# Down and retention output products, weight sums and accumulators of a two-layer trunk regrouped

## The chip, the cores and the metric

One core of a Trainium2 chip runs the whole program. The engines are named as the profile names them: PE (TensorE, matrix products), DVE (VectorE), ACT (ScalarE), POOL (GpSimd) and SP (SyncE, which issues DMAs). The metric is the device time of one execution in microseconds; lower is better.

## The reference, cut to what matters

```
h = x                                            # 512 rows, 1024 columns
for i in range(2):
    hn = rmsnorm(h, mix_norm_g[i])
    h = h + (sgu_mixer(hn, ...) if i == 0 else retention(hn, ...))
    h = h + swiglu(rmsnorm(h, ffn_norm_g[i]), ffn_w_gu[i], ffn_w_down[i])
return rmsnorm(h, final_norm_g)

sgu_mixer: z = gelu(h @ w_in); u, v = split(z); v = layernorm(v)
           mixed = causal(w_s) @ v, per chunk of 128 rows and group; (u * (mixed + b)) @ w_out
retention: q, k, v, g = split(h @ w_in); 4 heads; (norm(scores(q, k) @ v) * silu(g)) @ w_out
           # w_out is 2048 x 1024
swiglu:    a, b = split(h @ w_gu); (silu(a) * b) @ w_down      # hidden 2816: w_down is 2816 x 1024
```

## The kernel before

Every product of two float32 matrices is made as three matmuls of rounded parts (`three`, L191 to L193): high by high, high by low and low by high. A weight arrives by a DMA that SP issues, as a tile of two k-tiles (128 x 2 x 512, 512 KB). `split` (L169, L170) copies its high part on ACT (`wh`) and subtracts on DVE for the low part (`wl`). All working tiles come from one pool of 38 buffers.

The program is a list of jobs that `pipeline` walks. Each job has a fetch (the DMA), a prep (the split) and a run (the matmuls). A fetch is written 8 weighted jobs ahead of its run, one that holds an accumulating DMA 12 ahead, and a prep 5 ahead. A scheduler then puts the instructions in a fixed order on each engine; an engine works through its own order and waits by semaphores.

Large products are made by `seven`: a 2 x 2 block product with seven half-size products (P1, P7, P6, Q4, P5, P2, P3) in place of eight. The weight side needs sums of blocks: P7 uses block 22 + 12, P6 that sum + 11, Q4 that sum + 21, and P5 uses 12 + 11. The left side needs such sums too (`combos`, made by DVE). A *step* is a pair of k-tiles in one product; each product has two steps, so a seven has 14 jobs. Seven is used for gate and up (`gu`, five units a layer, 24 matmuls of 256 columns a job), for v and g of each retention head (`vg`), for two thirds of the down product (`dn_0`, `dn_1`, 8 k-tiles each) and for half of the retention output (`ro0`, 8 k-tiles); the last three have 12 matmuls of 512 columns a job.

What is left of the down product (`dn_2`, 6 k-tiles: 4 of unit 4, 2 of the small first part `gl`) and of the retention output (`ro1`, 8 k-tiles) is made by `last_rows` with all eight block products, row chunk by row chunk, so that chunk 3 can be normalised while the others are still multiplied. Its accumulators are `ps_dn` and `ps_ro`. The same form makes the SGU output (`ps_so`).

Weight sums are made in two ways. In `gu`, DVE adds the blocks (L302) in the prep. In `vg`, `dn` and `ro0`, the sums of P7 and P5 are made by an accumulating DMA that POOL issues (L280) onto the loaded tile; P6 and Q4 are added by DVE.

PSUM is a pool of four tiles of 4 KB a partition, handed out by the scheduler as they come free.

In the SGU stage the order of code is: v's first half, its activation (`activate_v`, L703), v's second half, u's first half, `rowsum` (L799) with the bias sums `add_b` (L801), `mix` (L847) with `mx` (L849), u's second half, and the output projection.

Of the kernel before, what the change touches and what calls it, by code (L numbers as in the profile page):

```python
# [27 lines left out]
EARLY = 12  # L28
# [3 lines left out]
SUMS_X = ("P7", "P5")  # L32
SUMS_GU = ()
# [19 lines left out]
class Job:  # L53


    def __init__(self, fetch=None, prep=None, run=None, early=False):
        self.fetch, self.prep, self.run, self.early = fetch, prep, run, early


def pipeline(jobs):  # L60
    weighted = [j for j in jobs if j.prep is not None]
    n = len(weighted)
    e = f = p = 0
    done = 0
    for job in jobs:
        while e < n and e < done + EARLY:
            if weighted[e].early:
                weighted[e].fetch()
            e += 1
        while f < n and f < done + FETCH:  # L70
            if not weighted[f].early:
                weighted[f].fetch()
            f += 1
        while p < n and p < done + PREP:
            weighted[p].prep()
            p += 1
        if job.prep is not None:
            done += 1
        job.run()
# [3 lines left out]
def trunk(ctx, tc, x, positions, mix_g, ffn_g, fin_g, sgu_w_in, sgu_w_s, sgu_b_s, sgu_ln_g, sgu_ln_b,  # L83
# [8 lines left out]
    psp = ctx.enter_context(tc.tile_pool(name="psp", bufs=4, space=PSUM))  # L92
# [105 lines left out]
    def project_t(name, w, slices, evac, col_of=None, halves=False, mid=None):  # L198
# [30 lines left out]
        then(lambda: evac(ps))  # L229

    def project_n(name, w, slices, evac, col_of=None):
# [22 lines left out]
    PRODUCTS = ("P1", "P7", "P6", "Q4", "P5", "P2", "P3")  # L254

    def seven(name, w, groups, c1, c2, A, evac, mid=None, dma_sums=(), turned=False):
# [16 lines left out]

        def fetch(p, g, s, nk):
            def load(key, i, j):
                raw[key, g, s] = G(f"wr_{name}_{key}_{g}_{s}")
# [4 lines left out]

            if p == "P7":
                load("t", 1, 1)
                (onto if p in dma_sums else load)("t" if p in dma_sums else "o", 0, 1)
            elif p == "P1":
                load("b11", 0, 0)
            elif p == "Q4":
                load("b21", 1, 0)
            elif p == "P2":
                load("b21", 1, 0)  # L290
            elif p == "P5":
                load("b12", 0, 1)
                (onto if p in dma_sums else load)("b12" if p in dma_sums else "o", 0, 0)
            elif p == "P3":
                load("b22", 1, 1)

        def prep(p, g, s, nk):
            use = {"P1": "b11", "P7": "t", "P6": "t", "Q4": "t", "P5": "b12", "P2": "b21", "P3": "b22"}[p]
            extra = {"P7": "o", "P6": "b11", "Q4": "b21", "P5": "o"}.get(p)
            if extra and p not in dma_sums:  # L300
                d, o = raw[use, g, s][:, 0:nk, :], raw[extra, g, s][:, 0:nk, :]
                nc.vector.tensor_tensor(d, d, o, ALU.add)  # L302
            parts[p, g, s] = split(raw[use, g, s], f"{name}_{p}_{g}_{s}", nk)
# [22 lines left out]
        def run(i):  # L326
            p, (g, s, nk) = PRODUCTS[i // len(steps)], steps[i % len(steps)]
# [23 lines left out]
        for i in range(len(PRODUCTS) * len(steps)):
            p, st_ = PRODUCTS[i // len(steps)], steps[i % len(steps)]
            jobs.append(Job(lambda p=p, st_=st_: fetch(p, *st_), lambda p=p, st_=st_: prep(p, *st_), lambda i=i: run(i),
                            early=p in dma_sums))
# [51 lines left out]
    def into_x(p, acc, c):  # L406

        def plus(i, j, ps, op):
            q = X[:, 2 * i:2 * i + 2, j * T:(j + 1) * T]
            nc.vector.tensor_tensor(q, q, ps, op)  # L410

        if p == "P1":
            plus(0, 0, acc["X"], ALU.add)
        elif p == "P7":
            plus(1, 1, acc["Y"], ALU.subtract)
        elif p == "P6":
            plus(1, 0, acc["X"], ALU.add)
        elif p == "Q4":
            plus(1, 0, acc["Y"], ALU.add)
        elif p == "P5":  # L420
            plus(1, 1, acc["X"], ALU.subtract)
        elif p == "P2":
            plus(0, 0, acc["Z"], ALU.add)
        elif c == 1:
            plus(0, 1, acc["X"], ALU.subtract)

    lefts = {}

    def last_rows(name, w, raws, ready, mid=None):
# [48 lines left out]

        def start(kp, j):
# [9 lines left out]
        then(lambda: norm(3, ps[3]))  # L489
        for c in (2, 1, 0):  # L490
            then(lambda c=c: chunk(c, ends, (0,)))
            if c == 0:
                then(lambda: norm(0, ps[0], 0))
# [3 lines left out]
            then(lambda c=c: norm(c, ps[c], 1 if c == 0 else None))  # L497
        lefts[name] = left
# [23 lines left out]
    def rows_of(cols, dst, name):  # L522
# [11 lines left out]
        nc.vector.tensor_copy(dst, ps[:, 0, :])  # L534

# [583 lines left out]
```

## Time and profile before

| | |
|---|---|
| median of 3 runs | 1233.0 us (1232.68 to 1233.67) |
| the profiled execution | 1233.38 us |
| its span, first to last instruction | 1231.7 us |
| granted PE clock over the span | 0.999 |
| PE, DVE, ACT, POOL busy | 98%, 77%, 49%, 4% |

The span is what the trace covers; 1.7 us of the execution lie outside it. A busy share is the part of the span in which an engine ran an instruction; a weight load of PE runs beside its matmuls and is counted apart. Times in rows are microseconds, and a matmul's duration overlaps that of the next, so the pitch from start to start is what a matmul costs.

### The profile page before, as it was taken

To read this page: it belongs to the slowest core of one execution; us is meant where nothing else is said; L and a number is where in the kernel's file an instruction comes from. 1 tells how busy PE (TensorE), PEld (TensorE's weight loads), DVE (VectorE), ACT (ScalarE), POOL (GpSimd) and SP (SyncE) were. 2 spreads that over 40 slices of the span, in tenths; PEclk is the share of its full clock that TensorE was granted. 3 is DMA by queue.
4 is the path that set the end of the run, shared out by engine and by line. 5 is a ranking of instruction groups with operands and counts; after the bars stand their busy time and mean duration, and the time that the engine had idled before them with its cause. 6 is when DMAs were issued, how large, how long until landed. Compare 5 with 4: busy or idle time off the path is not lost.

```text
span 1231.7 us, 18116 instructions
## 1 busy us (share of the span) xinstructions
PE 1208.4 (98%) x7290; PEld 1079.0 (88%) x7290; DVE 946.9 (77%) x1092; ACT 608.5 (49%) x772; POOL 47.4 (4%) x49
## 2 busy tenths in 40 slices
PE   8999999999999999999999999999999999999997
PEld 6778899998999898988888888788899989998995
DVE  5599578879878976697483957996588799879864
ACT  4434356345544564556373545575454454446442
POOL 1000000000000001001000010100000100010000
PEclk9999999999999999999999999999999999999999
DMA  9312317766775767338174573665146667677711
GB/s 331 123 69 75 114 45 230 217 160 230 232 227 145 260 208 188 76 111 223 58 214 96 159 174 127 165 218 175 35 146 199 201 184 260 199 196 204 260 53 69
DMA packets 112868, 204.89 MB, mean 166 GB/s; under 512 B 7016, under 2 KB 20368, under 8 KB 112784
## 3 DMA queue, kind: packets, MB, share of 16 engines
q1 hardware_dynamic: 102864, 184.84, 45.9%
q0 software_dynamic: 9920, 18.90, 9.0%
q8 instruction: 57, 0.93, 0.3%
q14 instruction: 27, 0.22, 0.1%
HBM read 201.61 MB, written 2.10 MB: 165 GB/s over the span
## 4 chain that ended last, share of the span: by engine, by line
PE 86%; DVE 9%; ACT 3%; issue 2%; DMA 0%; SPq 0%; DVEq 0%; ACTq 0%
PE X_gu L193 6%; PE X_gu L192 6%; PE X_gu L191 6%; PE Y_gu L193 3%; PE Y_gu L192 3%; PE Y_gu L191 3%; PE X_vg L191 2%; PE X_vg L193 2%; PE X_vg L192 2%; PE ps_qk L192 2%; PE ps_qk L193 2%; PE ps_qk L191 2%; PE X_dn L191 2%; PE X_dn L192 2%; PE X_dn L193 2%
## 5 line engine op out<-in xcount | busy, mean ns | idle before, releaser
L170 DVE TENSOR_TENSOR wl_gu_P<-wr_gu_b,wh_gu_P 128x1024 fp32r<-128x1024 f32 x80 | 95.3, 1221 | 44.2 <-ACT wh_gu_P L169 43.7
L169 ACT ACTIVATE wh_gu_P<-wr_gu_b 128x1024 fp32r<-128x1024 f32 x80 | 80.3, 1050 | 8.0 <-PE X_dn L193 6.6
L169 ACT ACTIVATE wh_gu_P<-wr_gu_t 128x1024 fp32r<-128x1024 f32 x40 | 42.4, 1059 | 59.4 <-DVE wr_gu_t L302 58.2
L192 PE MATMUL ps_qk<-XL_r,wh_qk 128*128 128x512 f32 (+1 forms) x160 | 55.7, 348 | 0.6 <-DVE XL_r L584 0.6
L191 PE MATMUL ps_qk<-XH_r,wh_qk 128*128 128x512 f32 (+1 forms) x160 | 55.5, 349 | 0.0
L193 PE MATMUL ps_qk<-XH_r,wl_qk 128*128 128x512 f32 (+1 forms) x160 | 55.2, 348 | 0.0
L170 DVE TENSOR_TENSOR wl_gu_P<-wr_gu_t,wh_gu_P 128x1024 fp32r<-128x1024 f32 x40 | 48.1, 1220 | 4.6 <-ACT wh_gu_P L169 4.2
L170 DVE TENSOR_TENSOR wl_vg_P<-wr_vg_t,wh_vg_P 128x1024 fp32r<-128x1024 f32 x16 | 19.6, 1223 | 39.0 <-ACT wh_vg_P L169 37.8
L302 DVE TENSOR_TENSOR wr_gu_t<-wr_gu_t,wr_gu_b 128x1024 f32<-128x1024 f32 x40 | 47.6, 1218 | 0.1
L170 DVE TENSOR_TENSOR wl_vg_P<-wr_vg_b,wh_vg_P 128x1024 fp32r<-128x1024 f32 x32 | 38.2, 1221 | 10.0 <-PE X_vg L192 9.9
L191 PE MATMUL Y_gu<-xP7h_f,wh_gu_P 128*128 128x256 f32 x160 | 45.3, 283 | 0.0
L192 PE MATMUL Y_gu<-xP7l_f,wh_gu_P 128*128 128x256 f32 x160 | 45.3, 283 | 0.0
L193 PE MATMUL Y_gu<-xP7h_f,wl_gu_P 128*128 128x256 f32 x160 | 45.3, 283 | 0.0
L191 PE MATMUL X_gu<-xP6h_f,wh_gu_P 128*128 128x256 f32 x160 | 45.3, 283 | 0.0
L192 PE MATMUL X_gu<-xP6l_f,wh_gu_P 128*128 128x256 f32 x160 | 45.3, 283 | 0.0
L193 PE MATMUL X_gu<-xP6h_f,wl_gu_P 128*128 128x256 f32 x160 | 45.3, 283 | 0.0
L191 PE MATMUL Y_gu<-XH_f,wh_gu_Q 128*128 128x256 f32 x160 | 45.3, 283 | 0.0
L192 PE MATMUL Y_gu<-XL_f,wh_gu_Q 128*128 128x256 f32 x160 | 45.3, 283 | 0.0
L193 PE MATMUL Y_gu<-XH_f,wl_gu_Q 128*128 128x256 f32 x160 | 45.3, 283 | 0.0
L191 PE MATMUL X_gu<-xP5h_f,wh_gu_P 128*128 128x256 f32 x160 | 45.3, 283 | 0.0
L192 PE MATMUL X_gu<-xP5l_f,wh_gu_P 128*128 128x256 f32 x160 | 45.3, 283 | 0.0
L193 PE MATMUL X_gu<-xP5h_f,wl_gu_P 128*128 128x256 f32 x160 | 45.3, 283 | 0.0
(544 smaller groups left out, 4319.1 us busy)
## 6 DMA issues: line engine op xcount, KB each, us to landing
wr_gu_b<-in_ffn_w_gu SPq DMA_DIRECT2D x100, 512.0 KB, 3.8
wr_gu_o<-in_ffn_w_gu SPq DMA_DIRECT2D x40, 512.0 KB, 4.7
wr_dn_b<-in_ffn_w_down SPq DMA_DIRECT2D x40, 512.0 KB, 4.5
wr_vg_b<-in_ret_w_in SPq DMA_DIRECT2D x40, 512.0 KB, 4.2
wr_gu_t<-in_ffn_w_gu SPq DMA_DIRECT2D x20, 512.0 KB, 4.2
wr_qk<-in_ret_w_in SPq DMA_DIRECT2D x32, 256.0 KB, 4.1
wr_dn<-in_ffn_w_down SPq DMA_DIRECT2D x12, 512.0 KB, 4.1
wr_ro_b<-in_ret_w_out SPq DMA_DIRECT2D x10, 512.0 KB, 4.8
```

The costliest lines, as they stand in the source:

```text
L169: nc.scalar.activation(h, s, AF.Copy)
L170: nc.vector.tensor_tensor(l, s, f32(h), ALU.subtract)
L191: nc.tensor.matmul(o, ah, bh, start=start, stop=False, skip_group_check=True)
L192: nc.tensor.matmul(o, ah, bl, start=False, stop=False, skip_group_check=True)
L193: nc.tensor.matmul(o, al, bh, start=False, stop=stop, skip_group_check=True)
L302: nc.vector.tensor_tensor(d, d, o, ALU.add)
```

## The change

Four things change together.

1. `dn_2` and `ro1` are gone as `last_rows`. The second part of the down product is one seven of two groups (k-tiles 8 to 15, and the six of unit 4 and `gl`): four steps, 28 jobs, seven of them half as long. The retention output is one seven of two groups (16 k-tiles): four steps, 28 jobs. The normalisation of row chunks goes into the evacuations of these sevens (`into_x` with `norm`).
2. Weight sums by accumulating DMA, in place of DVE: `gu` and `vg` have P7 and P5 so, and Q4 is added onto P6's tile after P6's split. `dn_0` has P7, P6 (two adds, one after the other), P5 and Q4. `dn_1` and `ro` have P7 and P5, and P6 and Q4 are added onto the tile of the product before, after its split. An add is written 8 jobs ahead of its product, a second one onto the same tile 3 jobs earlier, and the load 2 earlier still; an add onto a split tile stands in that tile's prep.
3. The order of products is P1, P7, P6, P2, P5, Q4, P3 in `gu`, `vg` and `dn_0`; `dn_1` and `ro` keep the old one.
4. PSUM tiles are four fixed buffers, given out in the order of code, the longest free first (`ps_free`, `done`). `activate_v(0, ...)` becomes a job, so that it stands behind the first five preps.

Per step of seven jobs, DMAs of 512 KB, plain loads + accumulating adds:

| | before | after |
|---|---|---|
| gu | 8 + 0 | 5 + 3 |
| vg | 6 + 2 | 5 + 3 |
| dn_0 | 6 + 2 | 6 + 5 |
| dn_1 | 6 + 2 | 5 + 4 |
| ro | 6 + 2 (ro0) | 5 + 4 |

In all, 36 accumulating DMAs become 152, and matmuls of 512 columns fall by 60 (dn 36 over the two layers, ro 24).

```
-EARLY = 12
+ADD = 8
+STEP = 3
+LOAD = 2
...
-SUMS_X = ("P7", "P5")
-SUMS_GU = ()
...
+            if p in dma_sums:
+                n = len(bs) - 1
+                return [(ADD + STEP * (n - 1) + LOAD, first)] + [
+                    (ADD + STEP * (n - 1 - i), lambda b=b: add(p, b, g, s, nk)) for i, b in enumerate(bs[1:])]
...
             parts[p, g, s] = split(raw[p, 0, g, s], f"{name}_{p}_{g}_{s}", nk)
+            for q in onto:
+                if FROM[q] == p:
+                    add(p, BLOCKS[q][-1], g, s, nk)
...
     def PS(name, shape=(P, 2, T)):
-        return psp.tile(list(shape), F32, tag="ps", name=name)
+
+        s = ps_free.pop(0)
+        t = psp.tile(list(shape), F32, tag=f"ps{s}", name=name)
+        ps_held.append((t, s))
+        return t
+
+    def done(*tiles):
+
+        for t in tiles:
+            i = next(i for i, (u, _) in enumerate(ps_held) if u is t)
+            ps_free.append(ps_held.pop(i)[1])
...
-    activate_v(0, vps)
+    then(lambda: (activate_v(0, vps), done(*vps)))
...
+    def into_x(name, w, groups, A, ready=None, mid=None):
...
+            seven(name, w, groups, 0, T, A, evac, mid, ("P7", "P5"), onto=("P6", "Q4"))
+        else:
+            seven(name, w, groups, 0, T, A, evac, mid, ("P7", "P6", "P5"), order=LATER, onto=("Q4",))
...
-        down(1)
-        unit(4, {("P2", i): lambda i=i: lefts[f"dn{l}_2"](0, 1 - i) for i in range(2)})
-        last_rows(f"dn{l}_2", ffn_w_down[l], [(lambda i: he[i], [20, 21]), (lambda i: hq[4][i], t[4])], ready)
+        unit(3)
+        unit(4, {("P2", 1): lambda: A[1]("P1", 0), ("P5", 0): lambda: A[1]("P7", 0), ("P3", 0): lambda: A[1]("P6", 0)})
+        into_x(f"dn{l}_1", ffn_w_down[l], [(t[2], t[3]), ([16, 17, 20], [18, 19, 21])], A[1], ready)
...
-    last_rows("ro1", ret_w_out[0], [(lambda i, hd=hd: zq[hd][i], list(range(4 * hd, 4 * hd + 4))) for hd in (2, 3)],
-              normed("f1", ffn_g[1:2], raw_copy("f1")))
+    into_x("ro", ret_w_out[0], [(t[0], t[1]), (t[2], t[3])], outA, normed("f1", ffn_g[1:2], raw_copy("f1")),
+           {("P1", 1): heads[3][3], ("P7", 1): heads[3][2]})
```

**PE in the SGU stage.** `rowsum` and the `mix` tiles are PSUM tiles, and so are `ps_u_0` and `ps_u_1`, the accumulators of u; a number behind a name tells one tile from another. Before, PE has:

```order
L799 MATMUL rowsum<-wst,ones 128x512 x2
L847 MATMUL mix_783<-wst,v_0_324 128x128 x2
L847 MATMUL mix_783<-wst,v_0_329 128x128 x2
L847 MATMUL mix_795<-wst,v_0_324 128x128 x2
L847 MATMUL mix_795<-wst,v_0_329 128x128 x2
L191 MATMUL ps_u_0_833<-XH_in,wh_u_0_527 128x512
L192 MATMUL ps_u_0_833<-XL_in,wh_u_0_527 128x512
```

After, it has:

```order
L864 MATMUL rowsum<-wst,ones 128x512 x2
L913 MATMUL mix_783<-wst,v_0_393 128x128 x2
L913 MATMUL mix_783<-wst,v_0_398 128x128 x2
L913 MATMUL mix_996<-wst,v_1_545 128x128 x2
L913 MATMUL mix_996<-wst,v_1_550 128x128 x2
L913 MATMUL mix_795<-wst,v_0_393 128x128 x2
L913 MATMUL mix_795<-wst,v_0_398 128x128 x2
L913 MATMUL mix_1008<-wst,v_1_545 128x128 x2
L913 MATMUL mix_1008<-wst,v_1_550 128x128 x2
L913 MATMUL mix_783<-wst,v_0_393 128x128 x2
L913 MATMUL mix_783<-wst,v_0_398 128x128 x2
L913 MATMUL mix_795<-wst,v_0_393 128x128 x2
L913 MATMUL mix_795<-wst,v_0_398 128x128 x2
L203 MATMUL ps_u_0_833<-XH_in,wh_u_0_527 128x512
```

All eight groups of `mix`, in four tiles, now stand ahead of u's second half; before, two tiles stood ahead of it and the others behind its first accumulator.

**POOL's queue of accumulating DMAs at the first down product (`dn0_0`).** A name says which tile is added onto: before, `t` is P7's and `b12` is P5's, for each of the two steps; after, `P622` is the tile that was loaded with block 22 for P6. Before, these four are the program's first, and those of the second down product (`dn0_1`) follow:

```order
L280 DMA wr_dn0_0_t_0_0_2302<-in_ffn_w_down 128x2x512
L280 DMA wr_dn0_0_t_0_2_2338<-in_ffn_w_down 128x2x512
L280 DMA wr_dn0_0_b12_0_0_2502<-in_ffn_w_down 128x2x512
L280 DMA wr_dn0_0_b12_0_2_2543<-in_ffn_w_down 128x2x512
L280 DMA wr_dn0_1_t_0_0_3505<-in_ffn_w_down 128x2x512
```

After, twelve of gate and up (six a unit) stand ahead, and the first down product has ten:

```order
L295 DMA wr_dn0_0_P622_0_0_2315<-in_ffn_w_down 128x2x512
L295 DMA wr_dn0_0_P622_0_2_2348<-in_ffn_w_down 128x2x512
L295 DMA wr_dn0_0_P722_0_0_2350<-in_ffn_w_down 128x2x512
L295 DMA wr_dn0_0_P622_0_0_2315<-in_ffn_w_down 128x2x512
L295 DMA wr_dn0_0_P722_0_2_2389<-in_ffn_w_down 128x2x512
L295 DMA wr_dn0_0_P622_0_2_2348<-in_ffn_w_down 128x2x512
L295 DMA wr_dn0_0_P512_0_0_2532<-in_ffn_w_down 128x2x512
L295 DMA wr_dn0_0_P622_0_0_2315<-in_ffn_w_down 128x2x512
L295 DMA wr_dn0_0_P512_0_2_2590<-in_ffn_w_down 128x2x512
L295 DMA wr_dn0_0_P622_0_2_2348<-in_ffn_w_down 128x2x512
```

P6's two tiles get their first add, then the second beside P7's one, and last the one of Q4, beside P5's. POOL issues in this order, so that an add that waits (for its tile's load, for the add before onto it, or for the split) holds up those behind it.

**ACT at v's activation.** The tiles `wh_v` are the high parts of v's second half's weights. Before, ACT has:

```order
L173 ACTIVATE wh_v_3_246<-wr_v_3_244,mix_cols 128x512 x2
L670 ACTIVATE xq_294,ss_96<-X 128x1024
L703 ACTIVATE v_0_324<-ps_v_0_121,ry_n_2_318 128x512 x2
L703 ACTIVATE v_0_329<-ps_v_1_122,ry_n_2_318 128x512 x2
L173 ACTIVATE wh_v_0_373<-wr_v_0_357,mix_cols 128x512 x2
L173 ACTIVATE wh_v_1_379<-wr_v_1_359,mix_cols 128x512 x2
```

After, it has:

```order
L185 ACTIVATE wh_v_3_246<-wr_v_3_244,mix_cols 128x512 x2
L735 ACTIVATE xq_294,ss_96<-X 128x1024
L185 ACTIVATE wh_v_0_363<-wr_v_0_347,mix_cols 128x512 x2
L185 ACTIVATE wh_v_1_369<-wr_v_1_349,mix_cols 128x512 x2
L185 ACTIVATE wh_v_2_375<-wr_v_2_351,mix_cols 128x512 x2
L185 ACTIVATE wh_v_3_381<-wr_v_3_353,mix_cols 128x512 x2
L185 ACTIVATE wh_u_0_387<-wr_u_0_355,mix_cols 128x512 x2
L768 ACTIVATE v_0_393<-ps_v_0_121,ry_n_2_318 128x512 x2
L768 ACTIVATE v_0_398<-ps_v_1_122,ry_n_2_318 128x512 x2
```

The two activations of v have moved behind five weight copies.

## Rows read from the trace of the kernel before

**Rows 1.** The page's first part: busy us (share of the span), instructions, by engine.
```profile
PE 1208.4 (98%) x7290; PEld 1079.0 (88%) x7290; DVE 946.9 (77%) x1092; ACT 608.5 (49%) x772; POOL 47.4 (4%) x49
```

**Rows 2.** The page's chain that ended last: share of the span by engine.
```profile
PE 86%; DVE 9%; ACT 3%; issue 2%; DMA 0%; SPq 0%; DVEq 0%; ACTq 0%
```

**Rows 3.** TensorE's waits: us in total, times, longest us.
```profile
PE Y_dn L193 <- DVE h_Q4l L397: 2.5, 4, 0.6
...
PE ps_v L191 <- ACT wh_v L173: 2.0, 1, 2.0
...
PE ps_gl L192 <- DVE XL_f L584: 1.7, 4, 0.6
...
PE Y_ro L191 <- ACT wh_ro_P L169: 1.6, 1, 1.6
...
PE ps_dn L191 <- DVE X L554: 1.0, 1, 1.0
```

**Rows 4.** Windows: busy us of PE, PEld, DVE, ACT, POOL; PEclk, DMA share, GB/s.
```profile
185.00:265.00 80.00, 80.00 (x669) 80.00 (x668) 64.53 (x58) 40.97 (x41) 3.63 (x3) 1.00 0.67 206
...
266.00:307.00 41.00, 40.37 (x204) 34.02 (x203) 38.41 (x36) 20.91 (x22) 1.21 (x1) 1.00 0.73 216
```

**Rows 5.** The timeline of TensorE in the SGU output projection: start us, us.
```profile
149.68 0.39 PE L192 MATMUL ps_so<-wl_so,so_h 128*128 128x512 f32 x1
...
154.21 0.40 PE L191 MATMUL ps_so<-wh_so,so_h 128*128 128x512 f32 x1
```

**Rows 6.** TensorE's matmul groups of ps_dn and of ps_ro, by line: duration ns min/median/max.
```profile
L191 PE MATMUL ps_dn<-wh_dn,dn_h x96: 389/389/501, 466.5 to 1223.5; 128*128 128x512 f32 x96
...
L191 PE MATMUL ps_ro<-wh_ro,ro_h x64: 389/389/497, 838.2 to 883.1; 128*128 128x512 f32 x64
```

**Rows 7.** The timeline of PE at Q4 of the first down product: start us, us.
```profile
286.52 0.50 PE L192 MATMUL Y_dn<-wl_dn_Q,h_Q4h 128*128 128x512 f32 x1
...
287.65 0.50 PE L193 MATMUL Y_dn<-wh_dn_Q,h_Q4l 128*128 128x512 f32 x1 [0.63 <-DVE h_Q4l L397]
```

**Rows 8.** Groups by line and form, DVE and POOL: busy us, mean ns.
```profile
L302 DVE TENSOR_TENSOR wr_gu_t<-wr_gu_t,wr_gu_b 128x1024 f32<-128x1024 f32 x40 | 47.6, 1218 | 0.1
...
L280 POOL DMA_DIRECT2D wr_dn_t<-in_ffn_w_down x8 | 9.6, 1200 | 538.5 <-DVE wl_gu_Q L170 528.7 <-DMA wr_dn_t<-in_ffn_w_down 9.7
```

**Rows 9.** The timeline of PE and DVE at the SGU's mixing: start us, us.
```profile
86.28 1.95 PE L847 MATMUL mix<-wst,v 128*128 128x128 f32 x16
...
88.79 0.47 PE L191 MATMUL ps_u<-XH_in,wh_u 128*128 128x512 f32 x1 [0.56 <-DVE add_b L801]
...
86.48 2.16 DVE L801 SCALAR_TENSOR_TENSOR add_b<-rowsum,gains_cols,add_b 128x128 f32<-128x128 f32 x8 [1.37 <-PE rowsum L799]
...
88.56 0.68 DVE L833 TENSOR_TENSOR ur<-ps_u,R 128x512 f32<-128x512 f32 x1
...
89.16 1.40 DVE L849 SCALAR_TENSOR_TENSOR mx<-mix,gains_cols,add_b 128x512 f32<-128x512 f32 x2
...
91.07 1.42 DVE L838 TENSOR_TENSOR y<-u,mx 128x256 f32<-128x256 f32 x4
...
92.41 1.22 DVE L170 TENSOR_TENSOR wl_so<-wr_so,wh_so 128x1024 fp32r<-128x1024 f32 x1
```

**Rows 10.** The timeline of DVE at the end of the program: start us, us.
```profile
1221.92 1.41 DVE L1081 SCALAR_TENSOR_TENSOR o<-X,nf_dn,g_fin 128x512 f32<-128x512 f32 x2
...
1224.39 0.69 DVE L554 TENSOR_TENSOR X<-X,ps_dn 128x512 f32<-128x512 f32 x1 [1.06 <-PE ps_dn L193]
```

**Rows 11.** The page's DMA queues: packets, MB, share of the 16 engines' span.
```profile
q1 hardware_dynamic: 102864, 184.84, 45.9%
...
q0 software_dynamic: 9920, 18.90, 9.0%
```

**Rows 12.** The DMA issues: KB each, median us to landing.
```profile
wr_gu_b<-in_ffn_w_gu SPq DMA_DIRECT2D x100, 512.0 KB, 3.8
...
wr_dn_t<-in_ffn_w_down POOLq DMA_DIRECT2D x8, 512.0 KB, 9.2
```

More of the change, by code (lines that the diff above doesn't have):

```diff
@@ L53, with __init__ @@
 class Job:
-    def __init__(self, fetch=None, prep=None, run=None, early=False):
-        self.fetch, self.prep, self.run, self.early = fetch, prep, run, early
+    def __init__(self, fetch=None, prep=None, run=None):
+        self.run = run
+        self.steps = [] if prep is None else (fetch if isinstance(fetch, list) else [(FETCH, fetch)]) + [(PREP, prep)]
 def pipeline(jobs):
-    weighted = [j for j in jobs if j.prep is not None]
-    n = len(weighted)
-    e = f = p = 0
+    weighted = [j for j in jobs if j.steps]
+    leads = sorted({n for j in weighted for n, _ in j.steps}, reverse=True)
+    at = dict.fromkeys(leads, 0)
     done = 0
     for job in jobs:
[L66 to L77, printed above, removed]
+        for n in leads:
+            while at[n] < min(len(weighted), done + n):
+                for m, step in weighted[at[n]].steps:
+                    if m == n:
+                        step()
+                at[n] += 1
+        if job.steps:
             done += 1
@@ L297, in prep, with load @@
-        def prep(p, g, s, nk):
[L298 to L303, printed above, removed]
+        def load(p, b, g, s, nk):
+            raw[p, b, g, s] = G(f"wr_{name}_{p}{b}_{g}_{s}")
+            nc.sync.dma_start(raw[p, b, g, s][:, 0:nk, :], source(b, g, s, nk))
@@ L339, in run @@
                     evac(p, acc, None)
+                    if p in closes:
+                        done(acc[chain[p]])
             elif n < len(steps) - 2:
@@ L347, in run @@
                     evac(p, acc, c)
+                done(acc["X"])
             if mid and (p, n) in mid:
                 mid[p, n]()
[L351 to L354, printed above, removed]
+        for i in range(len(order) * len(steps)):
+            p, st_ = order[i // len(steps)], steps[i % len(steps)]
+            jobs.append(Job(fetch(p, *st_), lambda p=p, st_=st_: prep(p, *st_), lambda i=i: run(i)))
     def rows(k0, n):
@@ L492, in last_rows @@
             if c == 0:
-                then(lambda: norm(0, ps[0], 0))
+                then(lambda: add(0, 0))
             if c < 2:
@@ L496, in last_rows @@
             then(lambda c=c: chunk(c, ends, (1,)))
[L497 to L498 removed]
+            then(lambda c=c: add(c, 1 if c == 0 else None))
     def rsqrt_cols(src, n, scale, name):
```

222 lines of the change are left out of this document (135 added, 87 removed).

## The prediction

> **What bounds the kernel.** I read the busy shares first. TensorE (PE) runs 98% of the span, VectorE (DVE) 77% [rows 1]: the kernel is bound by PE, and less than 2% of the span can be won from waits. The chain that ended last says the same, with PE at 86% and DVE at 9% [rows 2]; the 9% are stretches where PE's next matmul came from a late DVE. The list of PE's waits then tells what can be won besides matmuls: Q4 of the down products four times for DVE's low part of a left side, the second half of v once for a weight copy on ACT, the retention output once, the four transposes ahead of a gate/up stage for `XL_f`, and the last chunk for DVE's addition into X [rows 3]. No large wait is put down to a weight's DMA, though the DMA engines are busy 67% and 73% of the time in gate/up and in the first down product [rows 4]. So matmuls taken away count in full, work taken from DVE counts only where PE waits for DVE, and DMA work added costs nothing until it makes a weight late.
>
> **Fewer matmuls.** Successive 512-column matmuls start 4.53 us apart over 20 of them, so one costs 0.2265 us [rows 5]. `ps_dn` has 96 matmuls on each of three lines, 144 a layer, and `ps_ro` 64 on each, 192 [rows 6]. In seven products, the six k-tiles of `dn_2` need 7/8 of 144 = 126, and the eight of `ro1` 168. That is 2 x 18 + 24 = 60 fewer, **-13.6 us**. They lie on PE's own path, so nothing hides this gain.
>
> **Q4's wait.** Between two matmuls of Q4 that should start 0.23 us apart stand 1.13 us [rows 7]: 0.9 us lost, four times [rows 3], 3.6 us. DVE was late because of its own weight additions for P6 and Q4 (L302, 1.22 us each [rows 8]). All of these go from the down products, and more than 0.9 us stood ahead of each Q4. **-3.6 us** (bounds 0 and -3.6: DVE's evacuations of PSUM into X stay). In gate/up DVE loses 60 additions, 73 us over the program, but PE does not wait for DVE there, so I take nothing.
>
> **Retention output.** Its P7 waited 1.6 us for ACT [rows 3]. With two groups, P1 has 24 more matmuls, 5.4 us, but the copy still stands behind a left-side copy on ACT which DVE feeds. I leave 0.4 of the wait: **-1.2 us** (bounds 0 and -1.6).
>
> **The SGU stage.** Two things change order. ACT's copies of v's next weights stand ahead of v's activation, so the 2.0 us wait for `wh_v` [rows 3] goes: -2.0 us. Against that, the fixed PSUM buffers put all mixing ahead of u's second half. Before, `ps_u` started 2.31 us after DVE had begun `add_b`, whose end it waited for [rows 9]. After, its buffer is that of a `mix` tile, free when DVE has read that tile a second time. By DVE's order that reading comes behind `add_b`, one `ur`, two `mx`, four `y`, a small operation and one `wl_so`. From the starts in [rows 9]: `add_b` 2.08 us, `ur` 0.60, `mx` 1.31, `y` 1.34, `wl_so` 1.14, the third `mx` 0.70, the small one an estimated 0.4, together 7.6 us. So u's second half starts 5.3 us later; but sixteen more mixing matmuls are done by then that used to come later, near 1.8 us (as many took 1.95 before, the overlap at their end included), so 3.5 us are lost. The output projection behind it needs DVE's `y` and ACT's copies, which slide too; I put 1 us on it (0 to 2). Net -2.0 + 3.5 + 1.0 = **+2.5 us** (from -2.0, if DVE runs so far ahead that `ps_u` loses nothing, to +5, if v's wait stays and the projection slides by 1.5).
>
> **Transitions and the tail.** Ahead of the first q/k product and of the second gate/up, the low part of the last transposed chunk is waited for, 0.4 us each as for `ps_gl` [rows 3]. The normalisation now hangs on evacuations with more DVE work between, a little more each, **+0.6 us** for both (0 to 2). At the end, DVE finishes two output pieces of another chunk, 1.41 us [rows 10], and by the new order such a pair stands ahead of the last addition into X, which was not held up before: **+1.0 us** (0 to 1.4).
>
> **DMA.** From the queues' shares of 1231.7 us [rows 11]: 45.9% for 184.84 MB is 1.60 us of all 16 engines for a 512 KB load; 9.0% for 36 accumulating ones is 3.08 us each, 1.92 times as much. Per step of seven products, with 168 matmuls of 256 columns at 80/669 us each [rows 4], a gate/up step is 20.1 us of PE; a down step of 84 matmuls is 19.0 us. Gate/up goes from 8 loads, 12.8 us (64%, and the window shows 67%) to 5 loads and 3 adds, 17.2 us (86%); `vg` comes to the same 17.2 us, 91% of 19.0. `dn_0` goes to 6 loads and 5 adds, 25.0 us in 19.0: **131%**. `dn_1` and `ro` come to 20.3 us, 107%. So the DMA engines fall behind in `dn_0` by 6.0 us a step, 12 us in all, and in `dn_1` and `ro` by about 1.3 us a step, 5 us in four.
>
> Whether PE feels it depends on the lead. An add is written 8 jobs ahead: 8 x 12 x 0.2265 = 21.7 us. An add lands 9.2 us after its issue [rows 12], the copy on ACT and the subtraction on DVE take an estimated 2.3 us (the latter as in [rows 8]), so some 10 us are left for a backlog that grows to 12 us only at the stage's end, where gate/up with its 86% follows and lets it shrink. P6, with two adds behind one another, has its load and first add earlier still. I take waits of **+1.0 us** in all (bounds 0 and 28: twice the 12 us of `dn_0`, and 4 us more behind them).
>
> The Trainium skill speaks against adds from POOL: its page "SBUF — State Buffer", section "SBUF: two separate sides", says that such a DMA's descriptors can't be written while DVE runs an operation in a two-port mode. Here POOL's issue of an add takes 1.20 us on the mean [rows 8], in stages where DVE is busy 81% to 94% of the time [rows 4]; the row shows no such stall. What it would make of the time stands with rival 2.
>
> **The sum.** Against the profiled execution of 1233.4 us: -13.6 - 3.6 - 1.2 + 2.5 + 0.6 + 1.0 + 1.0 = -13.3, so 1220.1; the median of the runs lies 0.4 us below that execution, so **1219.7 us**. The unknown small terms at their bounds, without the DMA's, give 1212 to 1228.
>
> **Rivals.** (1) *The DMA engines become the bound* (the other sign). In `dn_0` each step asks for 131% of them. If the backlog comes on top of one left by gate/up at 86%, or if contention stretches the landing beyond the 21.7 us of lead, every further microsecond of backlog is one of PE. It decides from a landing of about 19 us on, twice what [rows 12] shows. With the leads used up, 2 x 12 + 4 = 28 us less the 1.0 in the sum: about 1247 us; with half of it, 1233. For it: the sums above, the adds' double price. Against it: no wait for a weight's DMA now at 73%. (2) *Adds late in part.* In `dn_1` and `ro` an add onto a split tile can be issued only after that split, and POOL issues in order, so one waiting add holds the next ones. P6's add is written with P7's prep, 9 jobs or some 22 us ahead of P6's run; the split ahead of it (2.3), its landing (9.2) and its own split (2.3) take 14 us, and a queue of three adds of 3.08 us the rest. Waits of 1 to 2 us at some six places, in place of the 1.0 of the sum: 1225 to 1231 us. By the skill's rule the adds of a step would come later by up to 1.2 us each, 6 us for the five of `dn_0`; the time would be this rival's, and I count 0.03 of its chance to that. (3) *The SGU stage and the joints cost nothing*: DVE's freed time lets `ps_u` start in time and the tail stays: -13.6 - 3.6 - 1.6 - 2.0 + 1.0 gives 1213 us. (4) *The gains do not come*: `ro` and `dn_1` are closed by DVE's evacuations with norms, PE waits there for left sides as it did for Q4, 3 to 4 us in each of three sevens: 1229 to 1232 us.
>
> **How the numbers follow.** Forecast 0.54, rival 3 0.12, rival 2 0.14, rival 4 0.08, rival 1 0.12. A change of 0.2%, 2.5 us, is about what measuring this kernel can tell from none. Below 1230.5 lie the forecast, rivals 3 and 2 and a little of 4: 0.80; within 2.5 us of 1233 the rest of 4 and a half-sized rival 1: 0.08; above 1235.5 the rest of rival 1: 0.12. The range of 8 in 10 leaves out rival 1 and the upper part of 4, and the very lowest: 1213 to 1231.
>
> **What would show it.** Right: PE busy near 1194 us; no wait of Q4 for `h_Q4l`; `wh_v` gone from the waits; a new wait of `ps_u` of some 3 to 4 us for DVE's `mx`; q0 with about 79 MB at near 38% of the engines. Wrong: PE waits in `dn_0`, `dn_1` or `ro` for ACT's `wh_dn_P` or `wh_ro_P` whose releaser is a DMA (rivals 1, 2), or for DVE's `X` or left sides in the two-group sevens (rival 4).

## The result and the profile after

The changed kernel takes 1236.3 us in the median of 20 runs (1232.6 to 1238.6); the kernel before takes 1233.1 us in 20 runs beside it (1232.2 to 1234.4). The ratio is 1.0021, with a 95% interval of [1.0013, 1.0029]: slower by 0.2%, where 1.1% faster was forecast. The profiled execution took 1234.2 us with a span of 1232.5 us. One execution of one experiment below (PSUM as one pool) took 1975 us at a mean granted clock of 0.558, which nothing here explains, and is left out of its numbers.

The page of the changed kernel, its busy times, its DMA queues and its chain that ended last, against [rows 1], [rows 11] and [rows 2]:

```profile
PE 1198.6 (97%) x7230; PEld 1067.0 (87%) x7230; DVE 876.8 (71%) x1053; ACT 644.4 (52%) x832; POOL 184.6 (15%) x165
...
q0 software_dynamic: 40448, 77.63, 37.9%
q1 hardware_dynamic: 84176, 148.66, 35.8%
...
PE 74%; issue 7%; DMA 7%; DVE 5%; POOL 3%; ACT 2%; SPq 0%; POOLq 0%; DVEq 0%; ACTq 0%
```

PE has the 60 matmuls fewer and DVE is 70 us less busy. The accumulating queue q0 takes 37.9% of the DMA engines, as worked out ahead. But the chain now runs through DMA (7%), POOL (3%) and "issue" (7%), where before it had 2% of "issue" and none of the others. The waits of PE, against [rows 3] (us in total, times, longest us):

```profile
PE mix L913 <- DVE add_b L866: 2.2, 1, 2.2
PE ps_gl L204 <- DVE XL_f L648: 2.0, 4, 1.0
PE ps_gl L203 <- ACT XH_f L647: 2.0, 1, 2.0
PE X_dn L205 <- DVE h_P5l L427: 1.7, 4, 0.6
PE ps_u L203 <- DVE mx L915: 1.6, 1, 1.6
PE X_dn L203 <- ACT h_P5h L426: 1.4, 2, 0.7
PE X_ro L203 <- ACT z_P5h L426: 1.3, 1, 1.3
PE X_dn L204 <- DVE wl_dn_P L182: 1.3, 2, 0.8
PE ps_qk L203 <- ACT XH_r L647: 1.3, 1, 1.3
...
PE Y_ro L203 <- ACT sg L1085: 1.1, 1, 1.1
...
PE Y_dn L205 <- DVE h_Q4l L424: 0.9, 1, 0.9
```

The wait for `wh_v` is gone; Q4 waits once, not four times. In their place stand many small waits of the two-group sevens, for P5's left sides and weights. None of them names a DMA. One step further down, ACT's own waits do (three of the rows that name a DMA):

```profile
ACT wh_dn_P L181 <- DMA wr_dn_P<-in_ffn_w_down: 27.6, 12, 4.6
...
ACT wh_dn_Q L181 <- DMA wr_dn_P<-in_ffn_w_down: 13.8, 8, 3.0
...
ACT wh_ro_P L181 <- DMA wr_ro_P<-in_ret_w_out: 11.5, 4, 4.6
```

How a late add reaches PE is seen in ACT's timeline at P5 of dn_1 in the first layer (start us, us, in brackets the idle time before and what ended it), and in the chain of the same stretch:

```profile
464.58 1.06 ACT L181 ACTIVATE wh_dn_P<-wr_dn_P 128x1024 fp32r<-128x1024 f32 x1 [3.31 <-DMA wr_dn_P<-in_ffn_w_down]
465.55 1.04 ACT L426 ACTIVATE h_P5h<-h_S 128x1024 fp32r<-128x1024 f32 x1
468.63 1.06 ACT L181 ACTIVATE wh_dn_P<-wr_dn_P 128x1024 fp32r<-128x1024 f32 x1 [2.04 <-DMA wr_dn_P<-in_ffn_w_down]
472.62 1.06 ACT L181 ACTIVATE wh_dn_P<-wr_dn_P 128x1024 fp32r<-128x1024 f32 x1 [2.92 <-DMA wr_dn_P<-in_ffn_w_down]
473.58 0.83 ACT L426 ACTIVATE h_P5h<-h_S 128x768 fp32r<-128x768 f32 x1
```

```profile
459.16 13.36 DMA wr_dn_P<-in_ffn_w_down
472.62 1.07 ACT wh_dn_P L181
473.71 0.93 DVE wl_dn_P L182
474.85 0.96 DVE h_P5l L427
475.86 0.50 PE X_dn L205
```

An add issued at 459.16 landed 13.36 us later. ACT, which works in order, waited for it with the left side `h_P5h` queued behind the weight copy, and so did DVE with `h_P5l`; PE got both late. The chain has the same piece in the second layer (an add of 14.54 us), and in `ro` an add of 11.72 us with ACT's copy behind it. The windows, against [rows 4] (PE, PEld, DVE, ACT and POOL busy, PEclk, DMA share, GB/s), are the first `dn_0`, `dn_1` before and after its first 27 us, and `ro`. A DMA packet counts whole in the window in which it starts, so a full stretch can show a share just above 1:

```profile
265.00:310.00 45.00, 45.00 (x227) 38.25 (x226) 35.98 (x33) 22.52 (x23) 9.72 (x9) 1.00 1.05 266
...
420.00:460.00 40.00, 40.00 (x209) 34.42 (x209) 31.27 (x32) 17.31 (x21) 15.46 (x14) 1.00 0.97 204
460.00:505.00 45.00, 39.27 (x176) 29.83 (x175) 35.86 (x45) 30.91 (x49) 4.31 (x5) 1.00 0.98 281
800.00:885.00 85.00, 78.51 (x363) 63.04 (x363) 65.35 (x82) 54.60 (x86) 17.07 (x15) 1.00 0.95 236
```

In `dn_0`, where the forecast saw the highest load, the DMA engines are full for 45 us and PE does not wait at all. Around `dn_1` and in `ro` they are at 0.95 or more for 85 us each, and PE loses about 6 us in `dn_1` from 460 us on, and as much in `ro`.

To compare stages between kernels, I sum over the starts of PE's instructions in the trace how much later each comes than the pitch of its form (0.227 us for 512 columns, 0.172 for 384, 0.120 for 256, 0.112 for 128) after the one before. In us, for the three places where the sum changed much; "adds" are those of a step in `dn_1` and `ro`, and in the kernel before the first and third places take in `dn_2`, the second `ro1`:

| kernel | adds | dn_1, layer 1, with the heads behind | ro, with gl behind | dn_1, layer 2 | median of runs |
|---|---|---|---|---|---|
| before | 2 | 4.9 | 4.1 | 2.6 | 1233.1 |
| changed | 4 | 10.7 | 10.5 | 5.7 | 1236.3 |
| changed, second profile | 4 | 11.1 | 11.4 | 6.0 | (1234.9, one run) |
| adds as plain writes | 4 | 3.1 | 3.2 | 1.1 | 1212.9 |
| P6, Q4 by DVE there | 2 | 3.3 | 12.9 | 2.7 | 1224.9 |
| all sums as before | 2 | 4.2 | 16.3 | 2.7 | 1230.4 |
| P6 by DMA, Q4 by DVE there | 3 | 5.1 | 3.1 | 5.9 | 1222.2 |
| Q4 by DMA, P6 by DVE there | 3 | 11.9 | 17.7 | 4.5 | 1241.3 |
| gate/up by DVE | 4 | 11.8 | 14.6 | 5.1 | 1237.8 |
| other order there | 4 | 11.2 | 9.0 | 10.3 | 1237.6 |
| P5's adds earlier | 4 | 12.2 | 16.3 | 8.6 | 1242.4 |
| dn_1 by DVE, ro P6 by DMA | 2, 3 | 3.3 | 3.0 | 2.7 | 1217.5 |

Over the whole program the lateness grew from 29.5 to 43.0 us in the two profiled executions, 13.5 us: the 13.6 us of the matmuls were won and lost again.

### The profile page after: what moved, and what is told of

Its sections match the earlier page's. It is cut to its first block, busy times and chain, and to the rows that moved or that the text cites. A ratio compares the mean times of both kernels' runs of the same rounds, so it can differ in the third digit from the quotient of the medians.

```text
span 1232.5 us, 18153 instructions
## 1 busy us (share of the span) xinstructions
PE 1198.6 (97%) x7230; PEld 1067.0 (87%) x7230; DVE 876.8 (71%) x1053; ACT 644.4 (52%) x832; POOL 184.6 (15%) x165
## 3 DMA queue, kind: packets, MB, share of 16 engines
q0 software_dynamic: 40448, 77.63, 37.9%
## 4 chain that ended last, share of the span: by engine, by line
PE 74%; issue 7%; DMA 7%; DVE 5%; POOL 3%; ACT 2%; SPq 0%; POOLq 0%; DVEq 0%; ACTq 0%
PE X_gu L205 6%; PE X_gu L204 6%; PE X_gu L203 6%; DMA wr_dn_P<-in_ffn_w_down 4%; PE Y_gu L205 3%; PE Y_gu L204 3%; PE Y_gu L203 3%; PE ps_qk L204 2%; PE ps_qk L205 2%; PE ps_qk L203 2%; PE X_vg L204 2%; PE X_vg L203 2%; PE X_vg L205 2%; POOL wr_dn_P L295 2%; PE X_dn L205 2%
## 5 line engine op out<-in xcount | busy, mean ns | idle before, releaser
L182 DVE TENSOR_TENSOR wl_gu_P<-wr_gu_P,wh_gu_P 128x1024 fp32r<-128x1024 f32 x120 | 143.3, 1220 | 48.1 <-ACT wh_gu_P L181 48.1
L181 ACT ACTIVATE wh_gu_P<-wr_gu_P 128x1024 fp32r<-128x1024 f32 x120 | 122.3, 1051 | 54.9 <-DVE wr_gu_P L323 35.7
L295 POOL DMA_DIRECT2D wr_gu_P<-in_ffn_w_gu x60 | 72.2, 1253 | 449.7 <-DVE wl_gu_P L182 142.1
L182 DVE TENSOR_TENSOR wl_dn_P<-wr_dn_P,wh_dn_P 128x1024 fp32r<-128x1024 f32 x72 | 79.9, 1132 | 16.1 <-ACT wh_dn_P L181 16.1
L181 ACT ACTIVATE wh_dn_P<-wr_dn_P 128x1024 fp32r<-128x1024 f32 x72 | 68.7, 978 | 33.1 <-DMA wr_dn_P<-in_ffn_w_down 27.6
L295 POOL DMA_DIRECT2D wr_dn_P<-in_ffn_w_down x52 | 60.1, 1201 | 162.7 <-DMA wr_dn_P<-in_ffn_w_down 68.2
L182 DVE TENSOR_TENSOR wl_vg_P<-wr_vg_P,wh_vg_P 128x1024 fp32r<-128x1024 f32 x48 | 57.3, 1221 | 26.7 <-ACT wh_vg_P L181 26.5
L181 ACT ACTIVATE wh_vg_P<-wr_vg_P 128x1024 fp32r<-128x1024 f32 x48 | 49.0, 1057 | 2.3 <-DVE wr_vg_P L323 1.6
L204 PE MATMUL X_gu<-XL_f,wh_gu_P 128*128 128x256 f32 x160 | 45.3, 283 | 0.0
L203 PE MATMUL Z_gu<-XH_f,wh_gu_P 128*128 128x256 f32 x160 | 45.3, 283 | 0.0
```

The lines of the kernel that those rows point to most:

```text
L181: nc.scalar.activation(h, s, AF.Copy)
L182: nc.vector.tensor_tensor(l, s, f32(h), ALU.subtract)
L203: nc.tensor.matmul(o, ah, bh, start=start, stop=False, skip_group_check=True)
L204: nc.tensor.matmul(o, ah, bl, start=False, stop=False, skip_group_check=True)
L295: nc.gpsimd.dma_start(raw[p, 0, g, s][:, 0:nk, :], source(b, g, s, nk), accum_op=ALU.add)
```

## The experiments

Theory A: the adds, at twice the engine time of a load, fill the DMA engines in the two-group sevens. Theory B: the order of DVE's and ACT's work in the new evacuations is what PE waits for. Theory C: POOL's queue, where one waiting add holds the next. Later, A is split: A1, the average load of a step counts; A2, two sets of adds fall on one stretch and compete. The median of the kernel before was 1232.7 to 1232.9 us beside each group of runs.

**The changed kernel again.**

> The changed kernel, untouched, for a second look. Its executions lie between 1232.6 and 1238.6 us and their mean granted clock between 0.991 and 0.998. Theory A (DMA engines are at capacity in the two-group sevens): the same stages wait as in the first profile, dn_1 and ro, by about as much (dn_1 of the first layer near 9 us, ro near 10, dn_1 of the second near 6), and what an execution has over the first profile's 1234.2 us stands in these stages or in a stretch with a lower clock behind one of them. Theory B (order of DVE and ACT in the evacuations with norms): the waits are the same to 0.2 us in both profiles.

1234.9 us; the same three stages wait, 11.1, 11.4 and 6.0 us. They are not the same to 0.2 us, but the differences are small, and the largest, in `ro`, stands at a stretch of 3.4 us with a lower clock (from 882.4 us on). This run alone does not decide between A and B.

**Adds as plain writes.** The same transfers from the same queue in the same order, without adding.

```
-            nc.gpsimd.dma_start(raw[p, 0, g, s][:, 0:nk, :], source(b, g, s, nk), accum_op=ALU.add)
+            nc.gpsimd.dma_start(raw[p, 0, g, s][:, 0:nk, :], source(b, g, s, nk))
```

> The adds of weights are plain writes from the same queue, in the same order and with the same waits (the weight sums are left out of the computation). Theory A: a transfer takes 1.6 us of the 16 DMA engines in place of 3.1, the two-group sevens ask for about 76% of them in place of 107%, their waits shrink by 10 to 13 us, 1222 to 1226 us. Theory B: the waits stay, 1233 to 1238 us. Theory C (POOL's queue in order, each add held by the one ahead): landings stay late by the waits of POOL, at most 3 us gained, 1231 to 1236 us.

1212.9 us, ratio 0.984 [0.983, 0.985]: 23 us faster than the changed kernel, more than A expected. Its queues on the page:

```profile
q1 hardware_dynamic: 84176, 148.66, 36.3%
q0 software_dynamic: 21504, 77.63, 19.6%
```

and its landing times (KB each, median us):

```profile
wr_dn_P<-in_ffn_w_down POOLq DMA_DIRECT2D x44, 512.0 KB, 6.2
```

The same 77.63 MB take 19.6% of the engines in place of 37.9%, and land in 6.2 us in place of 8.7. In the three places of the table 19.5 us of lateness are gone, and the stages wait less than before the change. B and C fall as the main cause: the order on every engine, POOL's too, is the same row for row. The run takes away the price of adding as a whole: besides the engine time, the packets of q0 fall from 40448 to 21504, and POOL's issue of one transfer from 1.20 to 1.25 us on the mean to 0.70 to 0.73.

**P6 and Q4 by DVE in dn_1 and ro.**

```
-            seven(name, w, groups, 0, T, A, evac, mid, ("P7", "P5"), onto=("P6", "Q4"))
+            seven(name, w, groups, 0, T, A, evac, mid, ("P7", "P5"))
```

> In dn_1 and ro alone, the sums of P6 and Q4 are made by DVE as they were before the change; P7 and P5 stay with the DMA. Theory A: a step asks for 6 loads and 2 adds, 15.8 us in 19.0; the waits for late adds go, DVE's 1.2 us for each sum cost a part of it again, 1224 to 1229 us. Theory B: DVE has some 10 us more to do in each of three stages where it is late already, 1238 to 1246 us.

1224.9 us, 0.994 [0.992, 0.995], within A's range. `dn_1` is late by 3.3 and 2.7 us, about as before the change. But `ro` has a new wait:

```profile
PE X_ro L203 <- ACT z_P6h L423: 8.4, 1, 8.4
```

There the last head's norm and products (L1105) stand in DVE's queue between its own weight sums (L323): four of these, at 1.2 us each, run from 798.5 us to the head's last product at 812.8. P6's left side needs that head. What follows is a chain through PE's transposes and ACT's copies, in which DVE itself stands idle for a while:

```profile
820.29 1.23 DVE L182 TENSOR_TENSOR wl_ro_P<-wr_ro_P,wh_ro_P 128x1024 fp32r<-128x1024 f32 x1 [6.74 <-ACT wh_ro_P L181]
```

So PE waits for DVE's and ACT's order in `ro` as soon as DVE makes the sums. In the changed kernel such a wait is small: `X_dn` for DVE's `X`, 0.8 us, which is there with plain writes too.

**All sums as before the change** (`onto` and `dma_sums` of gate/up, vg and dn_0 set back as well).

> All weight sums as before the change (gate/up by DVE alone, P7 and P5 by DMA elsewhere); the merged products, the order and the accumulators as in the changed kernel. Theory A: nothing is late by DMA; 60 matmuls fewer, 13.6 us, against 2 to 5 us of DVE waits: 1221 to 1226 us. Theory B: waits of the merged products stay or grow, 1234 to 1242 us.

1230.4 us, 0.998 [0.997, 0.999]: 4 us above A's range. `ro` waits again, 16.3 us with the stretch behind it, and 2.6 us stand at the joints for `XL_f` (1.1 in the run before). With the sums as they were, the change thus keeps 2.5 us of the 13.6 of its matmuls.

**Q4 by DMA only, and P6 by DMA only, in dn_1 and ro** (`onto=("Q4",)` and `onto=("P6",)`).

> In dn_1 and ro, P6's sum is made by DVE and Q4's by the DMA (5 loads and 3 adds a step, 17.2 us in 19.0 of the DMA engines, 91%). Theory A (capacity of the DMA engines): under 100% nothing piles up in dn_1, whose two stages wait 2 to 5 us in all in place of 15.7. In ro, DVE was seen to be late when it made both sums (8.4 us for z_P6h); with half of its sums I expect a wait of 2 to 6 us there. In all 1222 to 1227 us. If the landing of single adds counted and not the capacity, dn_1 would wait nearly as in the changed kernel: 1230 to 1236 us.

> The other half: P6's sum by the DMA, Q4's by DVE from a load of its own (6 loads and 3 adds a step, 18.8 us in 19.0, 99%). Theory A: between the changed kernel (107%) and the one with Q4 by DMA (91%), dn_1's two stages wait 5 to 11 us, 1226 to 1232 us. If only the number of adds counted, it would equal the other half.

1241.3 us (1.007 [1.006, 1.008]) and 1222.2 us (0.992 [0.990, 0.993]): the wrong way round for theory A by the average load of a step, 91% and 99%. Most of the difference is not a matter of the DMA engines' load alone: by the table 14.6 us of it stand in `ro`, where with P6's sum on DVE PE waits 6.4 us for `z_P6h` again. The first `dn_1`, with the heads behind it, makes 6.8 us, and the second is 1.4 us better with Q4 by DMA. The windows of both kernels at the first `dn_1`, and POOL's timeline of the one with Q4 by DMA, there and, in its last row, at the second:

```profile
434.00:450.00 16.00, 16.00 (x72) 13.24 (x71) 15.42 (x16) 5.23 (x6) 3.62 (x3) 1.00 0.40 97
450.00:470.00 20.00, 19.03 (x82) 15.13 (x81) 12.32 (x14) 9.70 (x11) 5.41 (x5) 1.00 1.09 249
```

```profile
434.00:450.00 16.00, 16.00 (x80) 13.58 (x79) 10.37 (x12) 5.96 (x7) 3.94 (x4) 1.00 0.98 218
450.00:470.00 20.00, 17.64 (x75) 13.67 (x74) 19.00 (x20) 10.24 (x12) 4.49 (x4) 1.00 1.06 292
```

```profile
444.75 1.19 POOL L295 DMA_DIRECT2D wr_dn_P<-in_ffn_w_down  x1 [18.27 <-DVE wl_dn_P L182]
446.50 2.44 POOL L295 DMA_DIRECT2D wr_dn_P<-in_ffn_w_down  x2 [0.56 <-DVE wl_dn_P L182]
452.93 2.12 POOL L295 DMA_DIRECT2D wr_dn_P<-in_ffn_w_down  x2 [4.00 <-DVE wl_dn_P L182]
456.00 1.20 POOL L295 DMA_DIRECT2D wr_dn_P<-in_ffn_w_down  x1 [0.96 <-PE X_dn L205]
459.34 1.19 POOL L295 DMA_DIRECT2D wr_dn_P<-in_ffn_w_down  x1 [2.14 <-issue]
461.00 0.91 POOL L295 DMA_DIRECT2D wr_dn_P<-in_ffn_w_down  x1 [0.47 <-issue]
...
1175.16 1.19 POOL L295 DMA_DIRECT2D wr_dn_P<-in_ffn_w_down  x1 [18.98 <-DVE wl_dn_P L182]
```

Q4's add goes onto P6's tile and can't be issued before DVE has added and split it. POOL sat 18.27 us waiting for that while the DMA engines were at 0.40, and then issued all eight adds of Q4 and P5 in 17 us; the changed kernel issues the same eight at the same time, from 444.29 us on. With P6's adds in place of Q4's the engines worked at 0.98 in the first stretch. This fits a rule that not the average counts, but how much add work is left in the stretch between its release and its use. It is not shown: at the second `dn_1` the same burst comes, eight adds within 17 us from 1175.16 us on after a wait of 18.98, and PE is late by 4.5 us there, against 5.9 with P6's adds. Even without the 3.4 us of lower clock that the latter has there, worth some 2 us, the two would be about equal.

**Gate and up by DVE again.**

> Gate and up alone with all sums by DVE again; everything else as changed. It takes the DMA engines from 86% to 64% in the stages ahead of dn_0 and dn_1 and leaves the two-group sevens at 107%. Theory A with the backlog made inside the two-group sevens: 0 to 3 us gained in dn_1, given back by DVE at the joints, 1233 to 1238 us. If the backlog is brought along from gate and up: dn_1's 15.7 us of waits fall below 6, 1224 to 1229 us.

1237.8 us, 1.004 [1.003, 1.005]. Nothing is gained in `dn_1` (11.8 and 5.1 us, against 10.7 and 5.7): the backlog is made there, and not brought along.

**Other orders with the same adds: P2 and P5 ahead of Q4 in dn_1 and ro (the first two lines of the excerpt); P5's load and adds 4 jobs earlier (its last line).**

```
-            seven(name, w, groups, 0, T, A, evac, mid, ("P7", "P5"), onto=("P6", "Q4"))
+            seven(name, w, groups, 0, T, A, evac, mid, ("P7", "P5"), order=LATER, onto=("P6", "Q4"))
...
+                ahead = ADD + (4 if p == "P5" and len(steps) > 2 else 0)
```

> dn_1 and ro take their products in the order P1, P7, P6, P2, P5, Q4, P3 too, with the same loads and adds (the norm of a chunk half waits for the later of its two parts). Theory A1 (a step's average load of the DMA engines counts): the 107% stay, 1233 to 1238 us. Theory A2 (the adds of Q4 and of P5 fall on one stretch: the split of P6 frees one set when the lead of 8 jobs asks for the other, eight adds in 17 us, and P5's land 13 us after issue): Q4's adds get 8 jobs more, so they no longer compete with P5's; waits of dn_1 and ro shrink from 26 us in all to 10 to 16, 1222 to 1228 us.

> The changed kernel with P5's load and add in dn_1 and ro 4 jobs earlier, nothing else; on POOL's queue two of P5's adds move ahead of two of Q4's. Theory A2 (late P5 adds): P5's first adds land some 8 us earlier, the waits for h_P5h and wh of P5 shrink, Q4's adds may become late in their place by 1 to 3 us; 1226 to 1234 us. Theory A1 (average load): no change, 1234 to 1238 us.

1237.6 us (1.003 [1.002, 1.005]) and 1242.4 us (1.008 [1.007, 1.009]). A2, that two sets of adds merely collide, falls: giving one of them more room makes another late. In the second, P5's waits in `dn_1` went, and Q4 waits in their place for its left side behind late tiles, 3.6 us in the two `dn_1` and 5.6 us in `ro`. None of the three orders tried carries four adds a step. The first of these two lies within A1's range, the second 4 us above it.

**The better of both for each place.**

```
+            seven(name, w, groups, 0, T, A, evac, mid, ("P7", "P5"), onto=("P6",) if name == "ro" else ())
```

> dn_1 with P6's and Q4's sums by DVE, ro with P6's by DMA and Q4's by DVE: the better one of two earlier runs for each place. If the stages add up, dn_1's two wait 4.5 us and ro 2.4 us as there, 5 us below the run with P6 by DMA in both: 1216 to 1220 us. If a gain in one stage is given back in the next, 1221 to 1225 us.

1217.5 us, 0.987 [0.986, 0.989]: the stages add up, and this beats the kernel before by 1.3% and the changed one by 1.5%.

**PSUM as one pool of four again**, in the changed kernel and in the better of both (`bufs=4` and one tag for all tiles).

> PSUM as one pool of four again, in place of four fixed buffers. If the fixed buffers cost what the prediction put on them in the SGU stage, ps_u starts some 3 to 4 us earlier after mix and the kernel gains 1 to 4 us, 1232 to 1235 us, with the other stages unchanged. If they cost nothing, 1235 to 1237 us.

> The kernel with P6's and Q4's sums by DVE in dn_1, and P6's by DMA in ro, with PSUM as one pool of four again. There no DMA is late, so that the accumulators' part can be seen. By the prediction's term, the fixed buffers cost 3.5 us where u's second half starts: 1213 to 1216 us with the pool. By the profile of the changed kernel with the pool, the wait moves to ps_u's other half and to v's second half: at most 1 us of 1217.5 changes, 1216.5 to 1218.5 us. If the fixed buffers help elsewhere (transposes, scores), the pool is slower: above 1219 us.

In the changed kernel 1238.2 us (1.004 [1.003, 1.006]; 1233.0 to 1242.2); its executions scatter so much that a difference of 1 to 3 us would not show, so this says little. In the better of both 1217.1 us (1216.3 to 1217.6), against 1217.5 (1216.7 to 1218.1): no difference to be told.

## Why the prediction was wrong

**The step that failed** is the last one of the part on the DMA, the wait that the leads leave over: "some 10 us are left for a backlog that grows to 12 us only at the stage's end", priced at +1.0 us. With plain writes in place of the adds the kernel is 23.4 us faster, so adding costs about that much, near the upper bound of 28 us that the text gave, and not its chosen value. The load per step was right (q0 at 37.9% where 38% was written); the place and the lead were not. The lead was counted in jobs of the code, and the landing taken from before, where a step had two adds. The add at 459.16 was issued 15 us ahead of its matmul, not 21.7, and took 13.36 us, not 9.2: when it was issued, three other adds and three loads were still under way. The eight adds of Q4 and P5 in this `dn_1` took 8.5 to 13.7 us, the eight ahead of them, P7's and P6's, 4.7 to 8.8.

As to the place: in the first `dn_0`, at 131% of the engines, the adds landed no faster, 6.2 to 12.0 us after issue, and yet PE did not wait. Its adds are written 8 to 11 jobs ahead, and the stage is over after 41 us. `dn_1` and `ro`, at 107%, are 67 and 76 us of PE long, and their adds all fall into the first five of seven products. That the longer lead and the shorter stage are what hid the backlog of `dn_0` is argued from these numbers; no run changed them alone.

**Rivals.** Rival 2, adds late in part, was right in the place and in the path (in-order engines behind a late tile) and too small: 1225 to 1231 us. Rival 1 gave the sign, but for `dn_0`. Rival 3, 1213 us, is near what the kernel is without the adds' price, 1212.9; that is in part chance, since of its terms the 2.0 us of the SGU stage did not come (0.3 by the sums of lateness) and the tail grew. Rival 4 had the sign that was seen: in the two-group sevens PE waits mostly for left sides, and hardly for `wh_dn_P` (0.4 us), which was to tell of the DMA. With plain writes, the order unchanged, these waits are gone, but for 0.8 us for `X`, so the sign pointed the wrong way. The chances at the end put the whole of rival 1 above 1235.5 us and count its half-sized form near 1233 once more.

**Matmuls**: right. There are 60 fewer, and 13.6 us show where little is late: the kernel with the better sums for each place is 15 us faster than before.

**Q4's wait**: right in mechanism. It is gone from `dn_0` in both layers; where adds are late it is back once, 0.9 us. With plain writes and with DVE's sums no wait of Q4 is left among PE's first ten.

**SGU stage**: the start of `ps_u` was right to 0.2 us, the sum was not. PE and DVE there, after:

```profile
86.39 3.81 PE L913 MATMUL mix<-wst,v 128*128 128x128 f32 x32 [2.24 <-DVE add_b L866]
91.84 0.50 PE L203 MATMUL ps_u<-XH_in,wh_u 128*128 128x512 f32 x1 [1.64 <-DVE mx L915]
```

```profile
84.09 2.15 DVE L866 SCALAR_TENSOR_TENSOR add_b<-rowsum,gains_cols,add_b 128x128 f32<-128x128 f32 x8
...
91.03 0.75 DVE L915 SCALAR_TENSOR_TENSOR mx<-mix,gains_cols,add_b 128x512 f32<-128x512 f32 x1
```

`ps_u` starts 7.75 us after `add_b`; 7.6 had been worked out from [rows 9]. `wh_v` is no longer waited for. Yet the stretch up to the projection's end is late by 14.4 us in place of 15.7: a gain of 1.3 where a loss of 2.5 was forecast. That gain is all in the first 14 us, 8.7 us late before and 7.4 after, and in the other runs, whose kernels begin alike, this part lies between 7.1 and 8.3. Behind it the lateness is 3.5, 1.9 and 1.5 us before (v; from v's end to the projection; the projection) and 0.5, 5.4 and 1.1 after. So v gained 3.0 us where 2.0 was forecast, the middle lost 3.5 as forecast, and the projection gained 0.4: together 0.1 us lost.

That the middle lost just 3.5 us is partly luck, for the fixed buffers do not explain it. With the pool of four in the better of both the middle is late by 5.8 us, with the fixed buffers by 5.4: there `ps_u` itself waits 2.2 us for `add_b`, and other waits come later. DVE is busy for 53 of the 58 us of this middle, before for 49 of 53; that it sets the pace there, and that time won in v comes back as waiting behind it, fits these numbers and was not tried by itself.

**Retention output**: P7's wait went from 1.6 to 1.1 us, where 0.4 was forecast. **Transitions**: +0.6 forecast; `ps_qk` and `ps_gl` wait 1.3 and 2.0 us for `XH` alone, which with plain writes they don't: part of the adds' price. **Tail**: from PE's last matmul to the end of the span 8.3 us in place of 7.3; right, with +1.0 forecast.

**DVE's freed time** was priced at nothing, since PE does not wait in gate/up. With all sums on DVE the kernel is 5.4 us slower than with those of `dn_1` and `ro` alone on it: part of that is at the joints, where DVE's `XL_f` comes later, part in `ro`. How it divides was not tried.

**The rule of the Trainium skill** ("SBUF — State Buffer", section "SBUF: two separate sides") that the descriptors of a DMA from POOL can't be written while DVE runs a two-port operation: no run here shows it. POOL's issue of an add takes 1.20 to 1.25 us on the mean, near the 1.20 of before, and with plain writes from the same queue the waits are gone. Whether DVE ran an operation of the kind that the rule names beside an add, no row here tells.

What stays open is whether any order carries four adds a step: two others were tried, and neither did. Open too is by what rule a set of adds comes late, the average load or the stretch that each has; the number of adds was never changed alone, with the places of the rest held.

## What to carry to other kernels

Price an added transfer by the engine time of its kind. Where the sum comes near what the engines can carry, a wait has wide bounds, and a value near the lower one needs a row that shows the lead. The average of a stage did not tell where PE would wait: here engines that were full for 45 us cost PE nothing, and at a lower forecast average, but full for 85 us, they cost it about 6 us in each place. When a late transfer is waited for by an in-order engine, look for its cost under the names of what stands behind it; no wait of PE in these sevens named a DMA. And when work is moved off a busy engine, try moving a part of it: the change with two of the four sums by DMA in `dn_1` and three in `ro` gained 1.3%, with all four in both it cost 0.2%.

## What was not expected of the hardware

The granted clock fell to its lower level, 1.2 GHz, for stretches of 3.4 to 13.7 us in kernels in which PE waited in the middle of the program. In the run with P6 and Q4 by DVE, around the wait of 8.4 us:

```profile
810.00:817.00 7.00, 7.00 (x38) 5.87 (x37) 3.52 (x6) 1.56 (x4) 2.12 (x2) 1.00 1.04 251
817.00:821.30 4.30, 0.71 (x7) 0.47 (x5) 1.01 (x1) 2.51 (x5) 1.20 (x1) 1.00 1.08 274
821.40:826.00 4.60, 0.00 (x0) 0.00 (x0) 3.53 (x4) 1.04 (x2) 1.21 (x1) 0.50 0.92 155
826.10:831.50 5.40, 5.36 (x12) 3.77 (x13) 5.37 (x5) 3.70 (x4) 0.00 (x0) 0.50 0.46 82
831.60:840.00 8.40, 8.40 (x38) 6.93 (x38) 8.40 (x9) 6.63 (x7) 0.00 (x0) 1.00 0.63 212
```

PE was idle from 817.7, the clock fell at 821.3 and came back at 831.5, so that the first twelve matmuls after the wait took 5.6 us in place of 2.7. A wait of 8.4 us thus costs about 11. In the kernel before, in the better of both and in the first profile of the changed kernel, the clock is at 2.4 GHz from 14 us to the end of PE's work; the second profile of the changed kernel has two stretches of 3.4 us at the lower level. The executions of the changed kernel have mean clocks between 0.991 and 0.998, which may be part of its wider scatter.
